# Six contraction groups instead of nine, with every accumulation on VectorE, and weight tiles split in one step of 2048 columns

## Chip, cores and metric

The kernel runs on one core of a Trainium2 chip. The metric is device time in microseconds of one execution of the whole layer, as the median of several runs. A profiled execution of its own gives the trace.

## What is computed

One layer of a streaming encoder on x of 256 tokens by 2048 columns, all in float32: a feed-forward block (FFN 1), a mixer of two attention branches, a second feed-forward block (FFN 2) and a last norm. Each of the three blocks has a norm ahead of it whose scale and shift, and a gate whose size, come from a vector c through one large matrix (`w_ada`, 2048 by 9 x 2048). The part that matters here is FFN 1:

```python
mod = (jax.nn.silu(c) @ w_ada[i] + b_ada[i]).reshape(B, N_MOD, D)
sh1, sc1, ga1, sh2, sc2, ga2, sh3, sc3, ga3 = [mod[:, j, None, :] for j in range(N_MOD)]
h = _rms_norm(x, g_ffn1[i]) * (1.0 + sc1) + sh1
x = x + 0.5 * ga1 * _swiglu(h, w1_a[i], w3_a[i], w2_a[i])     # (silu(h @ w1) * (h @ w3)) @ w2, D_FF = 5632
```

So h needs two of the nine parts of `mod` before its first row can be used, and w1 and w3 (2048 by 5632 each) are read once from HBM.

## The kernel before

**Exact products.** Every weight tile and every left operand is split into a high part that TensorE's float32r takes without loss and a remainder. `split_raw` (lines 87 to 102) does this for weights: ScalarE (ACT) copies a piece of the raw tile into `wh` (line 97), VectorE (DVE) subtracts it from the raw tile into `wl` (line 98). A tile of 2048 columns is taken in two pieces of 1024, each in buffers of its own; the pool `hl` has six of each kind. `mm3` (lines 108 to 111) then adds three products into PSUM: high by high (109), high by remainder (110), remainder by high (111). One "unit" of weights is 128 partitions by 2048 columns, 1 MB: four rows of tiles of 512 columns, for two blocks of 128 tokens, so 24 products of 128 by 512.

**Loads.** Raw tiles come through SyncE's (SP's) DMA queue into three buffers of 2048 columns (pool `raws`), in order. A buffer is free when its last reader is done: for a weight tile the DVE subtraction.

**Modulation.** `mod` is computed on DVE beside all this: an ada unit (lines 159 to 164) loads 1 MB of `w_ada` into a raw buffer, multiplies it by silu(c) and sums each row (line 163), which gives one column of one of the nine parts. `mod_cols` (201 to 213) turns columns into the scale and shift of the norm with three tiny DVE operations (208, 210, 212). `fill` issues queued ada units, `need` all up to a given one.

**The prologue of FFN 1** (lines 396 to 513). The first 6 of 11 chunks of 512 columns of w1 and w3 are done while `mod` is still arriving. The contraction over the 16 row tiles of h is cut into groups: `GROUPS = (1, 1) + (2,) * 7`. A group's rows of h^T are built when its ada units are done (`xn_T`, `mod_T`; the remainder of h is subtracted on GpSimd (POOL) here, line 312 with `early`). Then for each chunk and each of w1, w3 the group's products go into a PSUM tile `pacc`, one of two (`psA`), and from there into a running sum in SBUF, `sum`. That is 12 partial sums per group of 128 by 1024 elements, 108 in all:

- group 0: ACT stores the 12 sums (line 496);
- later groups: every third is added by DVE straight from PSUM (line 503); for the others ACT copies PSUM to `ev` (507) and POOL adds `ev` to `sum` (508), 56 in all;
- last group: the sum of w1 goes by ACT and POOL (500, 501) and then through silu on ACT (510), the sum of w3 by DVE, and POOL multiplies the two (512).

A raw tile of the prologue holds four slots of 512 columns, so 48 tiles in all. `AHEAD` says how many raw tiles ahead of its group the ada units of that group are issued; between these marks `target` spreads them evenly. 37 ada units belong to the prologue. Behind it `RATE = 0.75` ada units are issued per weight unit until the queue is empty.

**After the prologue** FFN 1 goes on with `ffn_down` for the six chunks, `ffn_up` and `ffn_down` for the other five (lines 515 to 523), then mixer and FFN 2. All of them take their weights through `gemm`, `unit_parts` and `split_raw`.

**What sets the order.** The source gives an order, and the framework that builds the program puts the instructions of each engine into a queue in the order in which they become ready by its own reckoning, those earlier in the source first; semaphores enforce the data's order. The queues are fixed when the program is built, and each engine works through its own strictly in that order.

Of the kernel before, what the change touches and what calls it, by code (L numbers as in the profile page):

```python
# [32 lines left out]
# offsets of the columns of `cols`  # L33
C_BADA, C_GF1, C_GMX, C_GF2, C_GQL, C_GKV, C_GQN, C_GKN = 0, 144, 160, 176, 192, 196, 200, 201
# offsets of the parts of `rows`
# [4 lines left out]
def layer_kernel(ctx: ExitStack, tc: tile.TileContext, a: dict):  # L40
# [6 lines left out]
    hl = ctx.enter_context(tc.tile_pool(name="hl", bufs=6, reuse_waits="tile"))  # L47
# [10 lines left out]
    def wkA(name):  # L58
        return wk.tile([P, 1024], F32, tag="wA", name=name)
# [4 lines left out]
    # ------------------------------------------------------------ constants  # L64
# [16 lines left out]
    # ------------------------------------------------------------ weights  # L81
# [5 lines left out]
    def split_raw(raw, src_cols, n):  # L87
        """exact parts of raw[:, :src_cols], as pairs of n columns"""
        res = []
        per = max(1, (src_cols // n) // 2)  # L90
        k = 0
        while k * n < src_cols:
            w = min(per * n, src_cols - k * n)
            wh = hl.tile([P, 1024], F32R, tag="wh", name="wh")
            wl = hl.tile([P, 1024], F32R, tag="wl", name="wl")
            src = raw[:, k * n:k * n + w]
            ACT.copy(wh[:, :w], src)  # L97
            DVE.tensor_tensor(wl[:, :w], src, wh[:, :w].bitcast(F32), op=ALU.subtract)  # L98
            for q in range(w // n):
                res.append((wh[:, q * n:(q + 1) * n], wl[:, q * n:(q + 1) * n]))  # L100
            k += w // n
        return res

    def unit_parts(ap, nkt, n):
        """one weight unit: nkt tiles of n columns"""
        return split_raw(load_unit(ap, nkt * n), nkt * n, n)
# [8 lines left out]
    def gemm(acc, units, n=512, tbm=None, mid=None, hook=None):  # L115
        """acc[tok, n] = x^T W over the units (ap, nkt, k0, xs); units tbm[0]:tbm[1] are
        done for one token block and then for the other"""
        total = sum(u[1] for u in units)
        tbm = tbm or (0, 0)
        i = 0  # L120
        held = []

        def run(tb, parts, i, xs, k0):
            for j, (wh, wl) in enumerate(parts):
                xh, xl = xs(k0 + j, tb)
                out = acc[tb][:, :n] if isinstance(acc, list) else acc[:, tb, :n]
                mm3(out, xh, xl, wh, wl, start=(i + j == 0), stop=(i + j == total - 1))

        for ui, (ap, nkt, k0, xs) in enumerate(units):
            if hook and ui in hook:  # L130
                hook[ui]()
            parts = unit_parts(ap, nkt, n)
            if tbm[0] <= ui < tbm[1]:
                held.append((parts, i, xs, k0))
                run(0, *held[-1])
                if ui == tbm[1] - 1:
                    if mid:
                        mid()
                    for h in held:
                        run(1, *h)  # L140
            else:
                for j, part in enumerate(parts):
                    if hook and j > 0 and ui + j / nkt in hook:
                        hook[ui + j / nkt]()
                    for tb in range(TB):
                        run(tb, [part], i + j, xs, k0 + j)
            i += nkt
            rate[1] += rate[0]
            while rate[1] >= 1.0:
                fill(1)  # L150
                rate[1] -= 1.0
        if hook and len(units) in hook:
            hook[len(units)]()

    # ------------------------------------------------------------ adaLN columns
# [15 lines left out]
    def need(j, kt):  # L171
        """issue what is queued up to the unit that gives column kt of mod j"""
        while (j, kt) not in ada_done:
            fill(1)
# [7 lines left out]
    def load_c(pool, first=False):  # L182
        """silu(c) on every partition"""
        c_bc = pool.tile([P, D], F32, tag="cbc", name="c_bc")
        if not first:
            ACT.dma_start(c_bc, a["c"].to_broadcast([P, D]))
            ACT.activation(c_bc, c_bc, AF.Silu)
            return c_bc
        SP.dma_start(c_bc[0:1, :], a["c"])
        ACT.activation(mod[:, 0:16], mhalf, AF.Silu)  # L190
        ps = bank("warm")
        for _ in range(WARM):
            PE.matmul(ps[:, 0:P], ones, ones, start=True, stop=True)
        ACT.activation(c_bc[0:1, :], c_bc[0:1, :], AF.Silu)
        for kg in range(4):
            ps = bank("c_ps")
            PE.matmul(ps, ones[0:1, :], c_bc[0:1, kg * 512:(kg + 1) * 512], start=True, stop=True)
            ACT.copy(c_bc[:, kg * 512:(kg + 1) * 512], ps)
        return c_bc

    def mod_cols(i, lo, hi, c_g):
        """columns lo:hi of (a, b) of norm i"""
# [12 lines left out]
    def gate_rows(pool, i, scale, name):  # L215
        """gate i as rows broadcast over the partitions, 512 columns at a time"""
# [25 lines left out]
    # ------------------------------------------------------------ norm into T layout  # L242
# [24 lines left out]
    def next_hT(i):  # L267
        """a list that takes h^T of norm i, and what fills it for a token block"""
        hT = []

        def then(tb):
            hT.append(new_hT_tb(tb))
            for kg in range(4):
                norm_T(hT, i, tb, kg * 4, 4)
        return hT, then
# [7 lines left out]
    def norm_T(hT, i, tb, k0, nk):  # L283
        """rows k0*128.. of h^T of norm i, in exact parts"""
        mod_T(hT, i, tb, k0, nk, xn_T(tb, k0, nk))
# [10 lines left out]
    def mod_T(hT, i, tb, k0, nk, ps, early=False):  # L296
# [15 lines left out]
        (POOL if early else DVE).tensor_tensor(lo, hv, hi.bitcast(F32), op=ALU.subtract)  # L312

    # ------------------------------------------------------------ FFN
    def ffn_act(acc1, acc3):
        """silu(acc1) * acc3"""
# [7 lines left out]
    def ffn_gT(g, ring, name):  # L324
        """g transposed, in exact parts: [P, 2, 4, S]"""
# [13 lines left out]
    def resid(acc, g, n, tbs, tail=False, then=None):  # L339
        """x += acc * gate for the 512 columns n of the token blocks tbs"""  # L340
# [13 lines left out]
    def add_product(units, g, n, tail, then, tbm, hook=None):  # L354
        """x += gate * (product) for the 512 columns n"""
# [39 lines left out]
    # ================================================================ FFN 1  # L395
    NPRO = 6
    GROUPS = (1, 1) + (2,) * 7
    ADD_DVE = 3
    LEAD = 3
    XLEAD = 1  # L400
    AHEAD = lambda gi: (0, 1, 0, 1, 2, 3, 4, 5, 5)[gi]
# [3 lines left out]
    with tc.tile_pool(name="f1", bufs=1, reuse_waits="tile") as f1, \  # L405
# [37 lines left out]
        # ada units that have to be issued before a raw tile  # L443
# [14 lines left out]
        for r, grp in enumerate(raws_of):  # L458
# [21 lines left out]
            for sl, part in zip(grp, split_raw(raw, len(grp) * 512, 512)):  # L480
                parts[sl] = part
            for gi, c, wi, k in grp:
# [12 lines left out]
                if gi == 0:  # L495
                    ACT.copy(sums[c][:, wi], acc)
                elif gi == len(GROUPS) - 1 and wi == 0:
                    pre = wkA("silu")
                    pv = pre.rearrange("p (t n) -> p t n", t=TB)
                    ACT.copy(pv, acc)  # L500
                    POOL.tensor_tensor(pv, pv, sums[c][:, 0], op=ALU.add)
                elif (c * 2 + wi) % ADD_DVE == 0 or gi == len(GROUPS) - 1:
                    DVE.tensor_tensor(sums[c][:, wi], acc, sums[c][:, wi], op=ALU.add)  # L503
                else:
                    ev = wkB("ev")
                    evv = ev.rearrange("p (t n) -> p t n", t=TB)
                    ACT.copy(evv, acc)  # L507
                    POOL.tensor_tensor(sums[c][:, wi], sums[c][:, wi], evv, op=ALU.add)  # L508
                if gi == len(GROUPS) - 1 and wi == 1:
                    ACT.activation(pre, pre, AF.Silu)  # L510
                    g = wkB("gact")
                    POOL.tensor_tensor(g, sums[c][:, 1].rearrange("p t n -> p (t n)"), pre, op=ALU.mult)
                    late.append(g)
# [12 lines left out]
    # ================================================================ mixer  # L526
# [16 lines left out]
    with tc.tile_pool(name="mx", bufs=1, reuse_waits="tile") as mx:  # L543
# [4 lines left out]
        with tc.tile_pool(name="mla", bufs=1, reuse_waits="tile") as ml:  # L548
            # ---- rotary tables
# [68 lines left out]
            # ---- latents  # L618
            def latent(parts, c_g, name):
                """RMS-normed latent, transposed, in exact parts; parts: per token block 512 columns"""  # L620
# [38 lines left out]
            # query latent, k_rope and g_lr: columns [q 0:256 | k_rope], [q 256:512 | g_lr]  # L659
# [13 lines left out]
            # ---- k_rope | g_lr  # L673
            def rope(dst, src, tab, nh):
                """dst, src [P, TB, nh, 64]"""
# [39 lines left out]
            def mla_pair(hp, k_hook):  # L715
                """latents up for two heads; returns the stages of their attention"""
# [136 lines left out]
        with tc.tile_pool(name="late", bufs=1, reuse_waits="tile") as lt, ExitStack() as ctx2:  # L853
# [5 lines left out]
            with tc.tile_pool(name="gla", bufs=1, reuse_waits="tile") as gl:  # L859
# [38 lines left out]
                def gla_head(h, hook):  # L898
                    """one head; returns the stages behind its projections"""
# [147 lines left out]
    # ================================================================ FFN 2  # L1047
# [37 lines left out]
def _units(w):  # L1085
    """[K, N] -> [K/512, N/512, 128, 4*512]: 512x512 blocks, rows k*128+p at partition p"""
# [59 lines left out]
```

## Time and profile before

| | us |
|---|---|
| median of 3 runs | 2260.61 |
| lowest and highest | 2259.78, 2260.78 |
| span of the profiled execution, first to last instruction | 2255.0 |
| prologue's products (`pacc`), first start to last start | 19.0 to 402.6 |
| TensorE, busy | 2161.3 (96%) |
| VectorE, busy | 1578.9 (70%) |
| ScalarE, busy | 1044.3 (46%) |
| GpSimd, busy | 276.6 (12%) |

The profiled execution is known by its span; what lies around a span counts in the runs' time. Busy time of TensorE is that of pipelined products and not a measure of its peak: the number of products in a window of time says more. Names: PE is TensorE, PEld its weight loads, DVE VectorE, ACT ScalarE, POOL GpSimd, SP SyncE. A group of instructions is named by line, engine, operation and by the tiles that it writes and reads; then come the count, the busy time, the mean duration in ns, and the idle time ahead of them with what ended it.

### The profile page before, as it was taken

To read this page: it belongs to the slowest core of one execution; us is meant where nothing else is said; L and a number is where in the kernel's file an instruction comes from. 1 tells how busy PE (TensorE), PEld (TensorE's weight loads), DVE (VectorE), ACT (ScalarE), POOL (GpSimd) and SP (SyncE) were. 2 spreads that over 40 slices of the span, in tenths; PEclk is the share of its full clock that TensorE was granted. 3 is DMA by queue.
4 is the path that set the end of the run, shared out by engine and by line. 5 is a ranking of instruction groups with operands and counts; after the bars stand their busy time and mean duration, and the time that the engine had idled before them with its cause. 6 is when DMAs were issued, how large, how long until landed. Compare 5 with 4: busy or idle time off the path is not lost.

```text
span 2255.0 us, 24933 instructions
## 1 busy us (share of the span) xinstructions
PE 2161.3 (96%) x9652; PEld 1763.1 (78%) x9652; DVE 1578.9 (70%) x1604; ACT 1044.3 (46%) x1279; POOL 276.6 (12%) x148
## 2 busy tenths in 40 slices
PE   8788788999999999999999999999999999999998
PEld 5566566788888887988777788878888888888886
DVE  6999898888787787756566667766666455444454
ACT  6545455433433445555564444455444433444443
POOL 1766557100000000001000000000000000000000
PEclk8899899999999999999999999999999999999999
DMA  8667675799898884644576777866777555555553
GB/s 297 230 233 253 227 248 192 276 352 347 334 336 324 328 318 148 227 145 165 195 256 245 257 262 278 296 235 241 281 287 268 191 208 196 189 193 187 194 189 112
DMA packets 87305, 549.16 MB, mean 244 GB/s; under 512 B 10322, under 2 KB 10626, under 8 KB 28435
## 3 DMA queue, kind: packets, MB, share of 16 engines
q1 hardware_dynamic: 84242, 539.97, 66.4%
q0 software_dynamic: 1344, 3.17, 0.5%
q10 hardware_dynamic: 1602, 4.44, 0.5%
q8 instruction: 75, 1.23, 0.2%
q14 instruction: 42, 0.34, 0.0%
HBM read 545.42 MB, written 2.12 MB: 243 GB/s over the span
## 4 chain that ended last, share of the span: by engine, by line
PE 82%; DVE 7%; issue 4%; DMA 3%; POOL 2%; ACT 1%; SPq 0%; POOLq 0%; DVEq 0%; ACTq 0%
PE a L109 10%; PE a L111 10%; PE a L110 10%; PE y L111 8%; PE y L110 8%; PE y L109 8%; DVE wl L98 3%; DMA raw<-in_w_a 2%; DVE raw L163 2%; POOL sum L508 1%; PE qkv L109 1%; PE ga L109 1%; PE gb L109 1%; PE ga L111 1%; PE qkv L111 1%
## 5 line engine op out<-in xcount | busy, mean ns | idle before, releaser
L98 DVE TENSOR_TENSOR wl<-raw,wh 128x1024 fp32r<-128x1024 f32 (+1 forms) x744 | 959.3, 1305 | 522.8 <-ACT wh L97 520.7
L97 ACT CAST wh<-raw 128x1024 fp32r<-128x1024 f32 (+1 forms) x744 | 765.5, 1042 | 965.2 <-PE a L111 283.7
L109 PE MATMUL a<-wh,hTh 128*128 128x512 f32 x1024 | 399.8, 390 | 0.3 <-ACT hTh L311 0.3
L111 PE MATMUL a<-wh,hTl 128*128 128x512 f32 x1024 | 399.0, 390 | 0.0
L110 PE MATMUL a<-wl,hTh 128*128 128x512 f32 x1024 | 398.6, 389 | 0.0
L163 DVE SCALAR_TENSOR_TENSOR raw<-raw,c_bc 128x2048 f32<-128x2048 f32 x144 | 351.1, 2438 | 38.1 <-DMA raw<-in_w_ada 37.7
L109 PE MATMUL y<-wh,gT 128*128 128x512 f32 x704 | 275.1, 391 | 0.0
L111 PE MATMUL y<-wh,gT 128*128 128x512 f32 x704 | 274.2, 389 | 0.0
L110 PE MATMUL y<-wl,gT 128*128 128x512 f32 x704 | 274.2, 389 | 0.0
L111 PEld LDWEIGHTS a<-wh,hTl 128*128 128x128 f32 x1024 | 192.2, 188 | 41.0 <-DVE hTl L312 0.8
L109 PEld LDWEIGHTS a<-wh,hTh 128*128 128x128 f32 x1024 | 192.3, 188 | 39.9 <-ACT hTh L311 0.6
L110 PEld LDWEIGHTS a<-wl,hTh 128*128 128x128 f32 x1024 | 192.3, 188 | 39.3
L109 PE MATMUL pacc<-wh,hTh 128*128 128x512 f32 x384 | 166.7, 434 | 56.0 <-DVE sum L503 50.1
L508 POOL TENSOR_TENSOR sum<-sum,ev 128x1024 f32<-128x1024 f32 x56 | 172.6, 3093 | 121.2 <-ACT ev L507 121.1
L110 PE MATMUL pacc<-wl,hTh 128*128 128x512 f32 x384 | 163.0, 424 | 11.3 <-DVE wl L98 11.3
L111 PE MATMUL pacc<-wh,hTl 128*128 128x512 f32 x384 | 161.0, 419 | 1.7 <-POOL hTl L312 1.7
L109 PEld LDWEIGHTS y<-wh,gT 128*128 128x128 f32 x704 | 132.2, 188 | 28.1
L111 PEld LDWEIGHTS y<-wh,gT 128*128 128x128 f32 x704 | 132.2, 188 | 27.3
L110 PEld LDWEIGHTS y<-wl,gT 128*128 128x128 f32 x704 | 132.2, 188 | 27.2
L109 PEld LDWEIGHTS pacc<-wh,hTh 128*128 128x128 f32 x384 | 79.4, 207 | 86.2 <-DVE sum L503 53.4
L507 ACT COPY ev<-pacc 128x1024 f32<-128x1024 f32 x56 | 56.8, 1014 | 106.1 <-PE pacc L111 100.6
L110 PEld LDWEIGHTS pacc<-wl,hTh 128*128 128x128 f32 x384 | 79.7, 207 | 29.9 <-DVE wl L98 13.8
(296 smaller groups left out, 2487.6 us busy)
## 6 DMA issues: line engine op xcount, KB each, us to landing
raw<-in_w_ada SPq DMA_DIRECT2D x144, 1024.0 KB, 5.2
raw<-in_w_b SPq DMA_DIRECT2D x132, 1024.0 KB, 4.8
raw<-in_w_a SPq DMA_DIRECT2D x84, 1024.0 KB, 5.8
raw<-in_w_in SPq DMA_DIRECT2D x60, 1024.0 KB, 4.8
raw<-in_w_a SPq DMA_DIRECT2D x84, 512.0 KB, 5.0
raw<-in_w_out SPq DMA_DIRECT2D x16, 1024.0 KB, 5.6
raw<-in_w_proj_a SPq DMA_DIRECT2D x8, 1024.0 KB, 4.9
raw<-in_w_proj_b SPq DMA_DIRECT2D x8, 1024.0 KB, 4.8
```

The lines of the kernel that those rows point to most:

```text
L97: ACT.copy(wh[:, :w], src)
L98: DVE.tensor_tensor(wl[:, :w], src, wh[:, :w].bitcast(F32), op=ALU.subtract)
L109: PE.matmul(out, xh, wh, start=start, stop=False)
L110: PE.matmul(out, xh, wl, start=False, stop=False)
L111: PE.matmul(out, xl, wh, start=False, stop=stop)
L163: DVE.scalar_tensor_tensor(out=raw, in0=raw, scalar=1.0, in1=c_bc, op0=ALU.mult, op1=ALU.mult, accum_out=dst)
L507: ACT.copy(evv, acc)
L508: POOL.tensor_tensor(sums[c][:, wi], sums[c][:, wi], evv, op=ALU.add)
```

## The change

Three things change together.

The groups become `(1, 1, 2, 4, 4, 4)`, with marks of their own for the ada units. The 48 raw tiles stay 48, the products stay the same in number; the partial sums fall from 108 to 72.

All partial sums behind group 0 are added by DVE straight from PSUM. In the last group, silu follows on ACT, and the product with it is DVE's. The remainder of h in the prologue is DVE's too. No tensor operation of the prologue is left on POOL but the powers of the norm.

`split_raw` takes one buffer pair of 2048 columns for a raw tile, three of each kind instead of six of half the size (the same memory), and splits it in one step: one ACT copy and one DVE subtraction of all its columns. Only the raw tiles of the first three groups are split in two steps, into that one buffer pair. This holds for all weights of the kernel.

```diff
-    hl = ctx.enter_context(tc.tile_pool(name="hl", bufs=6, reuse_waits="tile"))
+    hl = ctx.enter_context(tc.tile_pool(name="hl", bufs=3, reuse_waits="tile"))
...
-    def split_raw(raw, src_cols, n):
-        """exact parts of raw[:, :src_cols], as pairs of n columns"""
-        res = []
-        per = max(1, (src_cols // n) // 2)
-        k = 0
-        while k * n < src_cols:
-            w = min(per * n, src_cols - k * n)
-            wh = hl.tile([P, 1024], F32R, tag="wh", name="wh")
-            wl = hl.tile([P, 1024], F32R, tag="wl", name="wl")
-            src = raw[:, k * n:k * n + w]
-            ACT.copy(wh[:, :w], src)
-            DVE.tensor_tensor(wl[:, :w], src, wh[:, :w].bitcast(F32), op=ALU.subtract)
-            for q in range(w // n):
-                res.append((wh[:, q * n:(q + 1) * n], wl[:, q * n:(q + 1) * n]))
-            k += w // n
-        return res
+    def split_raw(raw, src_cols, n, steps=1):
+
+        wh = hl.tile([P, 2048], F32R, tag="wh", name="wh")
+        wl = hl.tile([P, 2048], F32R, tag="wl", name="wl")
+        w = src_cols // steps
+        for c in range(0, src_cols, w):
+            src = raw[:, c:c + w]
+            ACT.copy(wh[:, c:c + w], src)
+            DVE.tensor_tensor(wl[:, c:c + w], src, wh[:, c:c + w].bitcast(F32), op=ALU.subtract)
+        return [(wh[:, c:c + n], wl[:, c:c + n]) for c in range(0, src_cols, n)]
...
-        (POOL if early else DVE).tensor_tensor(lo, hv, hi.bitcast(F32), op=ALU.subtract)
+        DVE.tensor_tensor(lo, hv, hi.bitcast(F32), op=ALU.subtract)
...
-    GROUPS = (1, 1) + (2,) * 7
-    ADD_DVE = 3
+    GROUPS = (1, 1, 2, 4, 4, 4)
...
-    AHEAD = lambda gi: (0, 1, 0, 1, 2, 3, 4, 5, 5)[gi]
+    AHEAD = lambda gi: (0, 1, 1, 2, 4, 5)[gi]
...
-            for sl, part in zip(grp, split_raw(raw, len(grp) * 512, 512)):
+            for sl, part in zip(grp, split_raw(raw, len(grp) * 512, 512, 2 if GROUPS[grp[0][0]] < 4 else 1)):
...
-                elif gi == len(GROUPS) - 1 and wi == 0:
-                    pre = wkA("silu")
-                    pv = pre.rearrange("p (t n) -> p t n", t=TB)
-                    ACT.copy(pv, acc)
-                    POOL.tensor_tensor(pv, pv, sums[c][:, 0], op=ALU.add)
-                elif (c * 2 + wi) % ADD_DVE == 0 or gi == len(GROUPS) - 1:
-                    DVE.tensor_tensor(sums[c][:, wi], acc, sums[c][:, wi], op=ALU.add)
-                else:
-                    ev = wkB("ev")
-                    evv = ev.rearrange("p (t n) -> p t n", t=TB)
-                    ACT.copy(evv, acc)
-                    POOL.tensor_tensor(sums[c][:, wi], sums[c][:, wi], evv, op=ALU.add)
-                if gi == len(GROUPS) - 1 and wi == 1:
-                    ACT.activation(pre, pre, AF.Silu)
-                    g = wkB("gact")
-                    POOL.tensor_tensor(g, sums[c][:, 1].rearrange("p t n -> p (t n)"), pre, op=ALU.mult)
-                    late.append(g)
+                    continue
+                DVE.tensor_tensor(sums[c][:, wi], acc, sums[c][:, wi], op=ALU.add)
+                if gi == len(GROUPS) - 1:
+                    if wi == 0:
+                        pre = wkA("silu")
+                        ACT.activation(pre, sums[c][:, 0].rearrange("p t n -> p (t n)"), AF.Silu)
+                    else:
+                        g = wkB("gact")
+                        DVE.tensor_tensor(g, sums[c][:, 1].rearrange("p t n -> p (t n)"), pre, op=ALU.mult)
+                        late.append(g)
```

## The prediction

> **What bounds the kernel now.** The page comes first, for the shape of the run.
>
> ```profile
> span 2255.0 us, 24933 instructions
> ...
> PE   8788788999999999999999999999999999999998
> DVE  6999898888787787756566667766666455444454
> ...
> POOL 1766557100000000001000000000000000000000
> PEclk8899899999999999999999999999999999999999
> ```
>
> A slice is 56 us. After slice 7, PE is busy in full. Only in the first seven slices, the prologue that the change rewrites, is PE below that, while DVE is nearly full and POOL is in use, as almost nowhere later. A time table by stage says how far PE is from its best there.
>
> ```profile
> 300.00:350.00 50.00, 41.02 (x154) 32.46 (x155) 47.97 (x33) 24.03 (x29) 28.52 (x11) 0.88 0.70 237
> 500.00:550.00 50.00, 50.00 (x223) 41.28 (x222) 42.17 (x38) 19.18 (x20) 1.09 (x2) 1.00 0.92 355
> 850.00:900.00 50.00, 47.21 (x228) 37.90 (x226) 34.57 (x78) 30.83 (x56) 2.80 (x3) 1.00 0.40 136
> ```
>
> Columns: PE, PEld, DVE, ACT, POOL, each busy us with its count, then clock, DMA share, GB/s. A full window holds 223 products, one per 50 / 223 = 0.224 us; the prologue's window holds 154. DVE is busy 48 of 50 us there. The second window is the stage after the prologue: PE is full, but DMA is at 0.92 and 355 GB/s. Next come the groups of the first 410 us, by form.
>
> ```profile
> L98 DVE TENSOR_TENSOR wl<-raw,wh 128x1024 fp32r<-128x1024 f32 x101 | 191.4, 1922 | 23.2 <-ACT wh L97 23.1
> L508 POOL TENSOR_TENSOR sum<-sum,ev 128x1024 f32<-128x1024 f32 x56 | 172.6, 3093 | 121.2 <-ACT ev L507 121.1
> L109 PE MATMUL pacc<-wh,hTh 128*128 128x512 f32 x384 | 166.7, 434 | 56.0 <-DVE sum L503 50.1 <-ACT ev L507 4.2 <-ACT sum L496 0.9
> ...
> L163 DVE SCALAR_TENSOR_TENSOR raw<-raw,c_bc 128x2048 f32<-128x2048 f32 x38 | 108.7, 2861 | 5.9 <-DMA raw<-in_w_ada 5.8
> ...
> L503 DVE TENSOR_TENSOR sum<-pacc,sum 128x1024 f32<-128x1024 f32 x34 | 41.2, 1213 | 4.4 <-PE pacc L111 4.4
> ...
> L208 DVE TENSOR_TENSOR ab<-mod,small 128x2 f32<-128x2 f32 x7 | 10.4, 1484 | 0.1
> L212 DVE SCALAR_TENSOR_TENSOR ab<-modt,small 128x2 f32<-128x2 f32 x7 | 7.6, 1084 | 0.2
> ...
> L210 DVE TENSOR_TENSOR modt<-mod,small 128x2 f32<-128x2 f32 x7 | 5.4, 766 | 0.1
> ...
> L210 DVE TENSOR_TENSOR modt<-mod,small 128x1 f32<-128x1 f32 x2 | 0.3, 160 | 0.1
> ```
>
> PE's first product of a sum (L109) waits 50.1 us for DVE's addition, while DVE itself waits for little: 23.2 + 5.9 + 4.4 = 33.5 us. So DVE bounds the prologue. The odd part is its prices: a column operation on two elements takes up to 1.5 us where a like one, early on, takes 0.16. The lines of three instructions, first the split in the prologue, then split and modulation product (ada unit) after it, then the addition:
>
> ```profile
> L98 DVE TENSOR_TENSOR wl<-raw,wh x101: 1207/1227/3429, 17.9 to 407.9; 128x1024 fp32r<-128x1024 f32 x101
> ```
>
> ```profile
> L98 DVE TENSOR_TENSOR wl<-raw,wh x158: 1214/1219/1227, 419.4 to 848.1; 128x1024 fp32r<-128x1024 f32 x158
> ```
>
> ```profile
> L163 DVE SCALAR_TENSOR_TENSOR raw<-raw,c_bc x57: 2280/2284/2294, 424.0 to 832.8; 128x2048 f32<-128x2048 f32 x57
> ```
>
> ```profile
> L111 PE MATMUL pacc<-wh,hTl x384: 387/389/797, 20.1 to 402.6; 128*128 128x512 f32 x192
> ...
> L503 DVE TENSOR_TENSOR sum<-pacc,sum x34: 1209/1211/1225, 46.1 to 405.6; 128x1024 f32<-128x1024 f32 x34
> ```
>
> Durations are least/median/most in ns. Where POOL is idle, the split takes 1.22 us without exception; where POOL works, up to 3.43, which is the split plus most of a POOL addition (3.09 on average). The addition, which reads PSUM and one SBUF tile, never stretches (1.21 to 1.23) in the same stretch of time. I read this as POOL's additions holding up those DVE instructions that read two SBUF tiles.
>
> The Trainium skill, "SBUF — State Buffer", section "Who interferes with whom", states just that: DVE with two SBUF inputs and a GpSimd instruction that reads SBUF exclude each other, and the later one blocks in full. The trace agrees (3.43 against 1.22, and 1.21 flat for one SBUF input).
>
> **The prologue, part by part.** It lasts from 19 to 403 us, 384 us.
>
> (a) POOL's work goes: 56 sums, 6 + 6 of the last group, 18 remainders of h. The waits that it puts on DVE go with it: splits 191.4 - 101 x 1.22 = 68; ada units 108.7 - 38 x 2.284 = 22; columns 10.4 + 7.6 + 5.4 - 21 x 0.16 = 20. Together 110 us of DVE. What stays on POOL, the powers of the norms and the gate rows' DMAs behind the prologue, only loses predecessors.
>
> (b) DVE takes over. Six groups instead of nine leave 12 x 6 = 72 sums, 12 of them stored by ACT as now, 60 added on DVE: 26 more than the 34 now, at 1.21: 31.5 us. ACT's 56 evictions go as well; it was not the bound. The product with silu, 6 instructions:
>
> ```profile
> L321 DVE TENSOR_TENSOR gact<-a,silu 128x1024 f32<-128x1024 f32 x16 | 19.6, 1224 | 5.6 <-PE a L111 5.6
> ...
> L312 DVE TENSOR_TENSOR hTl<-hf,hTh 128x512 fp32r<-128x512 f32 x16 | 10.6, 685 | 2.4 <-ACT hTh L311 2.2
> ```
>
> 6 x 1.22 = 7.3. Remainders of h: 12 instructions over 4096 columns, between 8 x 0.685 = 5.5 by columns and 12 x 0.685 = 8.2 by count; I take 6. Sum added: 45.
>
> (c) Wide splits. A 2048-column split is not in the trace. Above stand two halves, 2.44 us; the nearest row is the ada unit, 2.284, of this width with two SBUF inputs. I take that: 36 wide tiles save 36 x 0.15 = 5.5. Three groups fewer save 9 column operations, 1.4.
>
> DVE then has 110 - 45 + 7 = 72 us less. If it waits as long as now, the prologue shortens by 72, to 312 us. PE needs 1152 products x 0.224 = 258 of these, so 83% where it is 67% now; the 48 + 37 tiles of 1.05 MB would need 286 GB/s where 355 are shown. With three engines near their limits waits grow: for a tile of the four-deep groups, PE needs 24 x 0.224 = 5.4 us and DVE 2.28 + 1.21 + half an ada unit 1.18 = 4.7, plus the small things. I add a third of today's DVE waits, 12 us; the ends are a third less and twice as much. **Prologue: -60 (from -84 to -38).**
>
> **After the prologue.** Between 420 and 850 us, every unit of four rows needs its own tile and about 0.7 of an ada tile from three buffers. Here is what SP's queue waits for, and how long tiles take to land when DMA is loaded (w_a) and when it is not (w_b).
>
> ```profile
> SPq L84 <- DVE wl L98: 239.8, 78, 5.7
> SPq L84 <- DVE raw L163: 121.2, 54, 7.0
> ```
>
> ```profile
> raw<-in_w_b SPq DMA_DIRECT2D x132, 1024.0 KB, 4.8
> raw<-in_w_a SPq DMA_DIRECT2D x84, 1024.0 KB, 5.8
> ```
>
> ```profile
> L97 ACT CAST wh<-raw 128x1024 fp32r<-128x1024 f32 x720 | 748.0, 1052 | 945.5 <-PE a L111 283.7 <-DMA raw<-in_w_a 241.1 <-PE y L111 180.3
> ```
>
> SP stands 361 of 430 us waiting for DVE to release a tile, so the loads run at the pace of the three buffers. A weight tile is released after half a copy and two half splits, 1.05 + 2.44 = 3.5 us; in one step it is a whole copy and a whole split. The copy of 2048 columns, which no row shows, takes more than one half, 1.05, and at most two, 2.10; near the upper end, as splits go by their columns. With 2.28 behind it that is 4.4 us at most: a weight tile is held up to 0.9 us longer. 158 half splits are 79 weight tiles, beside 57 ada tiles (the second and third of the lines above): 0.9 x 79 / 136 = 0.52 us in the mean, a third of it per transfer, x 136 = 24 us if nothing gives way. The lower end, a copy no longer than a half, would be a gain in holding (3.3 us against 3.5), which PE, full already, could not use: 0. What gives way: landing takes 5.8 us in this load and 4.8 without, so a thinner queue gives back up to 1.0 us, more than is lost; and PE is not short of anything here today. From 0 to 24, I take 8.
>
> Elsewhere DMA has room and PE's cover is thinner by half a tile. Where a chain of small steps runs between two stages (the window at 850 us, PE 47.2 of 50), ACT and DVE finish a piece of 2.1 to 2.3 us before they turn to it, not one of 1.05 to 1.22: half a microsecond more in the mean, at some four meetings. +2 (0 to 6).
>
> **Sum.** Against the profiled execution: 2255.0 - 60 + 8 + 2 = 2205 us of span. The median of the runs, 2260.6, is 5.6 above this span; that stays: 2210.6.
>
> **Rivals.**
>
> *Additions in the way (slower).* Every addition now stands on DVE and waits for PE. If the split of the next tile is queued behind the addition of the present one, PE and DVE take turns: 5.4 + 1.21 + 2.28 + 1.18 = 10.1 us for each of the 36 wide tiles, where the forecast has 324 / 48 = 6.75. That is +120, so 2331 us; from 15 of the 36 on (50 / 3.35) nothing is left of the gain. For it: the source has the steps in just this order. Against it: instructions do not stand on DVE as they do in the source.
>
> ```profile
> 188.37 3.48 DVE L98 TENSOR_TENSOR wl<-raw,wh 128x1024 fp32r<-128x1024 f32 x3
> 192.51 1.23 DVE L503 TENSOR_TENSOR sum<-pacc,sum 128x1024 f32<-128x1024 f32 x1 [0.66 <-PE pacc L111]
> ```
>
> Three half splits run before an addition that waits for PE: they are for later products. Three tiles of 2048 columns hold as many columns as six of 1024, so two tiles can lie ahead. Chance 0.15, mostly for parts of it.
>
> *Starved by the buffers.* The coarser release costs its full 24, the chains 6, and the prologue's waits double: -38 + 30 = -8, 2253 us. For it: SP's waits. Against it: the landing times. 0.10.
>
> *A slower PE clock.* The prologue has products of 797 ns beside 387 (the L111 line above) and a clock of 0.88. Waits for a whole tile are longer pieces of idleness; if a third of the products ran at half speed, PE alone would need 258 x 1.33 = 343 us, -41 instead of -60: 2230. The Trainium skill, "TensorE: Matmul & The Clock Gate", Part 1, says that an idle window of about 3.4 us halves the clock; by that rule a PE that waits more rarely would be faster, not slower. 0.03.
>
> *It does not do what it says.* If POOL is not what stretches DVE's instructions, 110 us stay and the added 45 come on top: -60 + 110 + 10 = +60, 2321 us. The flat 1.21 of the addition speaks against it. 0.02.
>
> **How the numbers follow.** The forecast has 0.70: about 2211, by itself from 2178 to 2248. The buffers' rival (0.10) lies at the upper end; both slower rivals (0.17) and a rest below are left out: 2178 to 2255. Some 0.2% (4.5 us) can be told from no change: the runs before lie within 1.0 us. Faster 0.70 + 0.03 + 0.06 of the buffers' rival = 0.79; same 0.04; slower 0.15 + 0.02 = 0.17.
>
> **What would show it.** The prologue's last product at about 343 us, not 403; splits of 2.28 us without stretched ones; column operations of 0.16 us; POOL empty; DVE still the busiest there. Additions found waiting for PE for long, with PE waiting for the split behind them, would show the first rival; PE below 50 of 50 us in the stage behind the prologue, with ACT waiting for DMA, the second. If splits stay stretched with POOL empty, the reading of the cause is wrong.

## The result, and the profile after

| | before | after |
|---|---|---|
| median of runs, us | 2260.2 (4 runs, 2259.13 to 2260.78) | 2207.6 (4 runs, 2202.86 to 2217.67) |
| ratio to before | 1 | 0.9768, 95% interval 0.9744 to 0.9793 |
| span of the profiled execution, us | 2255.0 | 2207.1 |

The change makes the kernel 2.3% faster. The page of the changed kernel, the same lines as before:

```profile
span 2207.1 us, 23664 instructions
...
PE   7799999999999989999999999999999999999998
...
DVE  7989887777777767555566677666665455444454
...
POOL 0000000000000000100000000000000000000000
PEclk9899999999999999999999999999999999999999
```

In the prologue PE is below nine tenths in two slices, not in seven, and POOL is empty; a new dent shows in slice 15. The tile `pacc`, its last product and the additions:

```profile
L105 PE MATMUL pacc<-wh,hTl x384: 387/389/629, 20.0 to 331.9; 128*128 128x512 f32 x192
L491 DVE TENSOR_TENSOR sum<-pacc,sum x60: 1208/1219/1225, 44.5 to 332.4; 128x1024 f32<-128x1024 f32 x60
```

The prologue's last product starts at 331.9 us instead of 402.6. Here are the groups up to 334 us, by form.

```profile
L95 DVE TENSOR_TENSOR wl<-raw,wh 128x2048 fp32r<-128x2048 f32 x38 | 87.0, 2288 | 14.0 <-ACT wh L94 13.8
L157 DVE SCALAR_TENSOR_TENSOR raw<-raw,c_bc 128x2048 f32<-128x2048 f32 x37 | 84.5, 2284 | 4.8 <-DMA raw<-in_w_ada 4.7
...
L491 DVE TENSOR_TENSOR sum<-pacc,sum 128x1024 f32<-128x1024 f32 x60 | 72.6, 1219 | 14.3 <-PE pacc L105 14.1
L95 DVE TENSOR_TENSOR wl<-raw,wh 128x1024 fp32r<-128x1024 f32 x24 | 28.8, 1218 | 3.6 <-ACT wh L94 3.6
...
L204 DVE TENSOR_TENSOR modt<-mod,small 128x4 f32<-128x4 f32 x3 | 0.5, 153 | 0.0
```

Nothing is stretched any more: the ada unit has 2.284 on average (2.861 before), the column operation 0.153 (0.766), the half split 1.218 (1.922). The wide split, which no row showed before, takes 2.288. DVE's waits in these four groups are 14.0 + 4.8 + 14.3 + 3.6 = 36.7 us, where the three of before had 33.5. Time by stage:

```profile
200.00:250.00 50.00, 49.45 (x217) 40.31 (x216) 45.25 (x35) 22.85 (x20) 0.00 (x0) 1.00 0.85 312
...
450.00:500.00 50.00, 49.51 (x218) 40.44 (x217) 36.65 (x24) 18.14 (x10) 0.00 (x0) 1.00 0.89 329
...
750.00:800.00 50.00, 47.22 (x200) 38.25 (x200) 33.54 (x26) 17.73 (x16) 0.00 (x0) 0.97 0.79 291
800.00:850.00 50.00, 44.59 (x226) 34.99 (x225) 38.85 (x108) 31.84 (x51) 1.81 (x3) 1.00 0.30 97
```

In the last part of the prologue PE now runs 217 products in 50 us, nearly the 223 of a full window. But the stage behind it, full before, now has 218, and the two windows around 800 us have PE busy for 47.2 and 44.6 of 50 us.

Behind the prologue, PE takes the products in the same order in all kernels of this study, but for six that change places between the 1173rd and the 1178th in after, wide_only and less_wide, and four there in dve_halves. So one can look up in each trace when PE starts the k-th (from 0) of the 2976 products with the low part of the weights; those of FFN 1 end with the 1055th. Differences to the kernel before, in us of their profiled executions:

| kernel | first behind the prologue (384th) | first of the mixer (1056th) | early in the mixer (1248th) | last (2975th) |
|---|---|---|---|---|
| after | -70.7 | -59.4 | -50.1 | -48.1 |
| groups_only | -74.7 | -74.7 | -74.8 | -74.1 |
| wide_only | +0.8 | +10.3 | +21.3 | +23.2 |
| nine_dve | -48.9 | -33.8 | -33.6 | -33.6 |
| two_steps | -71.5 | -71.4 | -70.0 | -69.4 |
| act_halves | -70.5 | -58.4 | -54.8 | -50.5 |
| dve_halves | -67.1 | -50.1 | -45.6 | -45.4 |
| less_wide | -70.3 | -69.4 | -60.3 | -57.3 |
| less_half | -71.0 | -70.9 | -70.1 | -70.1 |
| six_pool | -45.1 | -43.4 | -43.5 | -43.5 |
| pool_reads | -13.5 | -13.6 | -13.5 | -13.5 |
| pool_writes | -74.5 | -74.1 | -74.2 | -73.4 |

The changed kernel gains 70.7 us in the prologue and gives back 22.6 behind it: 11.3 up to the mixer's first product, 9.3 in the first part of the mixer, 2.0 in the rest.

### The profile page after: what moved, and what is told of

Its sections match the earlier page's. It is cut to its first block, busy times and chain, and to the rows that moved or that the text cites. A ratio compares the mean times of both kernels' runs of the same rounds, so it can differ in the third digit from the quotient of the medians.

```text
span 2207.1 us, 23664 instructions
## 1 busy us (share of the span) xinstructions
PE 2147.0 (97%) x9652; PEld 1749.7 (79%) x9652; DVE 1469.9 (67%) x1279; ACT 928.8 (42%) x845; POOL 39.0 (2%) x62
## 4 chain that ended last, share of the span: by engine, by line
PE 74%; DMA 9%; DVE 9%; ACT 4%; issue 3%; POOL 0%; SPq 0%; ACTq 0%; POOLq 0%; DVEq 0%
PE a L105 8%; PE a L104 8%; PE a L103 8%; DMA raw<-in_w_a 7%; PE y L105 6%; PE y L104 6%; PE y L103 6%; DVE wl L95 4%; ACT wh L94 3%; DVE raw L157 3%; PE pacc L104 2%; PE pacc L105 2%; PE pacc L103 2%; DMA raw<-in_w_ada 2%; PE qkv L103 1%
## 5 line engine op out<-in xcount | busy, mean ns | idle before, releaser
L95 DVE TENSOR_TENSOR wl<-raw,wh 128x2048 fp32r<-128x2048 f32 (+3 forms) x384 | 844.1, 2199 | 557.9 <-ACT wh L94 557.2
L94 ACT CAST wh<-raw 128x2048 fp32r<-128x2048 f32 (+3 forms) x384 | 705.8, 1839 | 1131.4 <-DMA raw<-in_w_a 392.8
L157 DVE SCALAR_TENSOR_TENSOR raw<-raw,c_bc 128x2048 f32<-128x2048 f32 x144 | 329.1, 2285 | 25.4 <-DMA raw<-in_w_ada 25.2
L103 PE MATMUL pacc<-wh,hTh 128*128 128x512 f32 x384 | 156.3, 407 | 14.5 <-ACT wh L94 8.7
L104 PE MATMUL pacc<-wl,hTh 128*128 128x512 f32 x384 | 155.9, 406 | 11.0 <-DVE wl L95 10.7
L105 PE MATMUL pacc<-wh,hTl 128*128 128x512 f32 x384 | 153.8, 400 | 0.0
L103 PEld LDWEIGHTS pacc<-wh,hTh 128*128 128x128 f32 x384 | 74.2, 193 | 36.7 <-ACT wh L94 10.8
L104 PEld LDWEIGHTS pacc<-wl,hTh 128*128 128x128 f32 x384 | 74.7, 194 | 32.2 <-DVE wl L95 17.1
L105 PEld LDWEIGHTS pacc<-wh,hTl 128*128 128x128 f32 x384 | 74.7, 194 | 15.4
L491 DVE TENSOR_TENSOR sum<-pacc,sum 128x1024 f32<-128x1024 f32 x60 | 72.6, 1219 | 14.3 <-PE pacc L105 14.1
```

The lines of the kernel that those rows point to most:

```text
L94: ACT.copy(wh[:, c:c + w], src)
L95: DVE.tensor_tensor(wl[:, c:c + w], src, wh[:, c:c + w].bitcast(F32), op=ALU.subtract)
L103: PE.matmul(out, xh, wh, start=start, stop=False)
L104: PE.matmul(out, xh, wl, start=False, stop=False)
L105: PE.matmul(out, xl, wh, start=False, stop=stop)
L157: DVE.scalar_tensor_tensor(out=raw, in0=raw, scalar=1.0, in1=c_bc, op0=ALU.mult, op1=ALU.mult, accum_out=dst)
```

## The experiments

Theory A: POOL's additions held up DVE, DVE bounds the prologue, and the wide split only costs. Rival B: the smaller number of sums is the gain. Rival C: the wide split is part of it.

**groups_only**: the two parts of the change kept apart.

```diff
-        wh = hl.tile([P, 2048], F32R, tag="wh", name="wh")
-        wl = hl.tile([P, 2048], F32R, tag="wl", name="wl")
...
+            wh = hl.tile([P, 1024], F32R, tag="wh", name="wh")
+            wl = hl.tile([P, 1024], F32R, tag="wl", name="wl")
```

(`split_raw` and the six buffers of before, all else as after.)

> The changed kernel with the split of before: two halves of 1024 columns in six buffers; groups 1,1,2,4,4,4 and all additions on DVE stay. Theory A (POOL's additions held up DVE, DVE bounds the prologue, the wide split only costs later): prologue's last product at 330 to 340 us, nothing lost behind it, so 2260 - 70 = about 2190 us, faster than the changed kernel by 15 to 20. Rival C (the wide split is a good part of the gain in the prologue): prologue's end at 350 or later, 2205 us or more.

Measured: 2182.55 us median (5 runs, 2181.13 to 2187.59), ratio to before 0.9656 (0.9643 to 0.967). It is the fastest kernel here, by 25 us ahead of the changed one. The last products of its prologue:

```profile
L111 PE MATMUL pacc<-wh,hTl x384: 387/389/628, 20.0 to 327.9; 128*128 128x512 f32 x192
```

The prologue is 4 us shorter with half splits, and next to nothing (0.6 us) is lost behind it. Rival C falls. The 4 us themselves are not firm: less_half, with the same splits and buffers but other ada units at the prologue's end, has -71.0 in the table, as the changed kernel has.

**wide_only**: the other part alone, on the kernel before.

```diff
-    hl = ctx.enter_context(tc.tile_pool(name="hl", bufs=6, reuse_waits="tile"))
+    hl = ctx.enter_context(tc.tile_pool(name="hl", bufs=3, reuse_waits="tile"))
...
+    def split_raw(raw, src_cols, n, steps=1):
```

> The kernel before with only the split changed: wide buffers, three of them, one step behind the prologue, two steps within it (all its groups are under four rows deep). Theory A: the prologue stays at its 403 us within 10 us, since POOL's additions stay; behind it the 20 to 25 us are lost that the changed kernel loses there, so 2280 to 2290 us. Rival C: a gain in the prologue, 2250 us or less.

Measured: 2277.17 us (4 runs), ratio 1.007 (1.0053 to 1.0087): 0.7% slower, 3 us less than theory A's range has. In its prologue, whose groups have one or two rows, every tile is split in two steps, so this run tests the one-step split behind the prologue only. The prologue stays (+0.8 us), 22.4 us are lost behind it, as much as in the changed kernel. There the one-step split is a loss by itself, and the same loss with or without the other part.

**nine_dve**: nine groups, no addition on POOL.

```diff
-    GROUPS = (1, 1, 2, 4, 4, 4)
+    GROUPS = (1, 1) + (2,) * 7
```

(on groups_only, with the marks of before)

> Groups 1,1,2,2,2,2,2,2,2 as before, half splits as before, but all 96 additions, the remainders of h and the product with silu on DVE and none on POOL. Theory A: the 110 us of stretched DVE instructions go, 62 additions of 1.21 us and 13 us of other work come, so DVE has 22 us less and the kernel takes about 2240 us (2225 to 2255). Rival B (the number of partial sums is what counts, POOL does not hold up DVE): DVE gets 62 x 1.21 + 13 = 88 us more, 2320 us or more.

Measured: 2220.11 us (4 runs), ratio 0.982 (0.9806 to 0.9833). Groups up to 410 us:

```profile
L98 DVE TENSOR_TENSOR wl<-raw,wh 128x1024 fp32r<-128x1024 f32 x116 | 138.5, 1216 | 13.3 <-ACT wh L97 13.2
L497 DVE TENSOR_TENSOR sum<-pacc,sum 128x1024 f32<-128x1024 f32 x96 | 115.9, 1218 | 11.1 <-PE pacc L111 10.8
```

DVE does 62 additions more and the kernel is faster all the same (1.8%), because the split is back at 1.216. Rival B in its strict form falls. The gain is larger than was expected, 48.9 us in the prologue where 22 were; of this DVE's waits give 12.4 (from 19 us to the prologue's end it is idle 20.3 us, 32.7 before). Its busy time there falls by 36.5 us (352.4 to 315.9) where 22 were expected; some 8 of the difference are work that it has not done yet at that point, three half splits and two ada units, and the rest was not followed up. And though it splits in halves, it gives back 15 us up to the mixer's first product. In that stretch its splits are ready 2 us ahead of PE in the median, those of groups_only 8 to 9. So time is lost there without any wide split too.

**six_pool**: the groups alone.

```diff
-    GROUPS = (1, 1) + (2,) * 7
+    GROUPS = (1, 1, 2, 4, 4, 4)
```

(on the kernel before, with the marks of after)

> The kernel before with the groups 1,1,2,4,4,4 alone: a third of the additions on DVE, the others by ACT and POOL, half splits. POOL's tensor operations fall from 234 to about 161 us. Theory A: three parts in ten of the 110 us of held-up DVE instructions go, 34 us, and 12 additions on DVE fewer, 15 us: about 2212 us (2195 to 2230). Rival B (the number of sums counts, whoever adds them): as groups_only, 2183 us.

Measured: 2214.74 us (4 runs), ratio 0.9799 (0.9783 to 0.9815), 2.7 above theory A's figure. Up to 410 us:

```profile
L98 DVE TENSOR_TENSOR wl<-raw,wh 128x1024 fp32r<-128x1024 f32 x116 | 179.3, 1576 | 40.3 <-ACT wh L97 40.3
L163 DVE SCALAR_TENSOR_TENSOR raw<-raw,c_bc 128x2048 f32<-128x2048 f32 x43 | 121.8, 2837 | 15.8 <-DMA raw<-in_w_ada 15.8
L508 POOL TENSOR_TENSOR sum<-sum,ev 128x1024 f32<-128x1024 f32 x32 | 93.2, 2915 | 141.2 <-ACT ev L507 141.1
```

With fewer POOL additions the split is stretched less (1.576, not 1.922; 1.616 for the 99 of the prologue alone, which ends at 357 us here). So groups alone bring 45 us in the prologue, no POOL alone 49, both together 75: they overlap, since fewer sums also means fewer POOL additions.

**pool_reads and pool_writes**: the disputed mechanism by itself.

```diff
+        spare = f1.tile([P, 512], F32, name="spare")
+        for q in range(112):
+            POOL.tensor_tensor(spare, x_sb[:, 0, 0:512], x_sb[:, 1, 0:512], op=ALU.add)
```

(on groups_only; pool_writes has 320 times `POOL.memset(spare, 1.0)` instead)

> Six groups, half splits, all additions on DVE (the kernel of groups_only, 2183 us), plus work on POOL that nobody waits for: 112 additions of two stretches of 512 columns of x in SBUF into a spare tile, about 1.5 us each by half of the 3.09 us row, 170 us in all, free to run from the start of the prologue. Theory A: splits and ada units are stretched while it lasts; before, 234 us of POOL's tensor operations gave 110 us of DVE waiting, so some 80 us here (40 to 110), nearly all of it on the path: 2225 to 2290 us. If POOL does not hold up DVE: 2183 us within 5.

> The same, but the extra POOL work only writes: 320 fills of 512 columns of the spare tile, some 0.5 us each, 160 us in all. If it is POOL's reading of SBUF that holds up DVE's instructions with two SBUF inputs, nothing changes: 2183 us within 5, splits at 1.22 us. If any POOL work does, as in pool_reads: 2220 us or more.

Measured: pool_reads 2243.52 us (4 runs), ratio 0.993 (0.9915 to 0.9945); pool_writes 2184.65 us (4 runs), ratio 0.967 (0.9654 to 0.9686). The groups up to 334 us, pool_reads first:

```profile
L458 POOL TENSOR_TENSOR spare<-x_sb 128x512 f32<-128x512 f32 x112 | 247.2, 2207 | 15.9 <-DMA x_sb<-in_x 7.3
L98 DVE TENSOR_TENSOR wl<-raw,wh 128x1024 fp32r<-128x1024 f32 x82 | 130.7, 1621 | 9.7 <-ACT wh L97 9.7
...
L163 DVE SCALAR_TENSOR_TENSOR raw<-raw,c_bc 128x2048 f32<-128x2048 f32 x34 | 99.5, 2925 | 0.0
L500 DVE TENSOR_TENSOR sum<-pacc,sum 128x1024 f32<-128x1024 f32 x50 | 60.2, 1214 | 4.5 <-PE pacc L111 4.3
```

```profile
L458 POOL MEMSET spare<- 128x512 f32 x320 | 168.6, 527 | 18.3
...
L98 DVE TENSOR_TENSOR wl<-raw,wh 128x1024 fp32r<-128x1024 f32 x102 | 122.1, 1219 | 13.5 <-ACT wh L97 13.0
...
L163 DVE SCALAR_TENSOR_TENSOR raw<-raw,c_bc 128x2048 f32<-128x2048 f32 x38 | 86.8, 2283 | 2.9 <-DMA raw<-in_w_ada 1.6 <-ACT c_bc L198 1.4
L500 DVE TENSOR_TENSOR sum<-pacc,sum 128x1024 f32<-128x1024 f32 x60 | 72.6, 1219 | 14.1 <-PE pacc L111 13.8
```

The split's least, median and most in ns, again pool_reads first:

```profile
L98 DVE TENSOR_TENSOR wl<-raw,wh x81: 1205/1224/2316, 27.2 to 329.8; 128x1024 fp32r<-128x1024 f32 x81
```

```profile
L98 DVE TENSOR_TENSOR wl<-raw,wh x102: 1211/1218/1226, 17.8 to 329.7; 128x1024 fp32r<-128x1024 f32 x102
```

Work on POOL that no one waits for costs 61 us if it reads SBUF: splits 1.621, ada units 2.925, and the addition with one operand in PSUM stays at 1.214. Work that only writes costs nothing measurable, with 169 us of it. A fill is shorter than an addition (0.53 against 2.2 us), but not one of the 102 splits beside the fills takes more than 1.226 us, so the difference is not one of length alone. Some 9 of the 61 us are another cause: the second block's power of the norm stands in POOL's queue behind six of the extra additions and starts at 23.2 us, and the prologue's first product starts at 28.1 us instead of 18.9. That POOL's additions, which read SBUF, hold up DVE's instructions with two SBUF operands, and its fills do not, is thus shown, not only argued. The Trainium skill, "SBUF — State Buffer", section "Who interferes with whom", draws the same line between a GpSimd instruction that reads SBUF and one that only writes it; these two runs agree with it (61 us and 2).

**two_steps, act_halves, dve_halves**: what the loss behind the prologue is.

```diff
-        return split_raw(load_unit(ap, nkt * n), nkt * n, n)
+        return split_raw(load_unit(ap, nkt * n), nkt * n, n, 2)
```

(two_steps, the prologue's call likewise; the other two take the halves for ACT's copy or DVE's subtraction alone. All have the three wide buffers.)

> The changed kernel with every tile split in two steps, but into the same three wide buffers. It tells apart what the loss behind the prologue (23 us) comes from. If the length of a piece on ACT and DVE counts (1.9 and 2.3 us instead of 1.05 and 1.22): most of the loss comes back, about 2190 us. If the coarser release of the split buffers counts: it stays, 2200 to 2210 us.

> The changed kernel, but ACT copies every weight tile in two halves; DVE subtracts it in one step as in the change, in the same three wide buffers. With both engines in halves 2187 us, with neither 2208. If the long pieces of ACT are what the small steps between the stages queue behind: most of the 20 us come back, 2187 to 2193. If those of DVE: little, 2203 to 2208. If both alike: about 2197.

> The mirror image: ACT copies a weight tile in one step, DVE subtracts it in two halves. If DVE's long pieces are what counts: 2187 to 2193 us. If ACT's: 2203 to 2208. If both alike: about 2197.

Measured: two_steps 2187.3 us (4 runs, ratio 0.967, 0.9657 to 0.9683), act_halves 2203.48 (4 runs, 0.975, 0.9733 to 0.9768), dve_halves 2212.11 (4 runs, 0.9783, 0.9763 to 0.9802). Halves on both engines bring nearly all of the loss back; halves on either engine alone bring back little or nothing. That was none of the three cases in the expectations. The effects do not add because a piece is not all that changes. With halves on both, DVE works on the first half while ACT copies the second: a raw tile is free 1.05 + 2 x 1.22 = 3.5 us after its copy starts. In the other three it is 1.91 + 2.29 = 4.2 (after), 2.10 + 2.29 = 4.4 (act_halves), 1.91 + 2.44 = 4.35 (dve_halves): ACT and DVE work one after the other. The traces bear this out: over the first 64 weight tiles behind the prologue the medians are 3.44, 4.24, 4.32 and 4.31 us. In the table, up to the mixer's first product, two_steps loses 0.1 us, the other three 11.3, 12.1 and 17.0. The coarser split buffers as such cost little: two_steps and groups_only are 4.7 us apart, and their intervals meet.

**less_wide and less_half**: is it the load on the raw buffers?

```diff
+    POOL.memset(mod, 0.0)
...
-            ada_q.append(lambda kt=kt: ada_unit(c_bc, j, kt))
+            if j in (2, 3, 4, 5) and kt % 2:
+                ada_q.append(lambda kt=kt: ada_done.add((j, kt)))
+            else:
+                ada_q.append(lambda kt=kt: ada_unit(c_bc, j, kt))
```

> The changed kernel with every second ada unit of parts 2 to 5 of the modulation left out (its column is zero), so that behind the prologue about half as many ada tiles share the three raw buffers. To be read against less_half, the same with half splits in six buffers. With all ada units the wide split costs 25 us (4 in the prologue, 21 behind it). If that is because a weight tile holds its raw buffer longer while loads run at the pace of the three buffers: with the load relieved, little is left of the 21, and the two kernels differ by 4 to 9 us. If the long pieces themselves stand in the way of the small steps between FFN 1 and mixer: the difference stays at 19 to 25 us.

> The kernel of groups_only (six groups, additions on DVE, half splits in six buffers) with the same ada units left out: PE was full behind the prologue there already, so 2175 to 2183 us by either theory.

Measured: less_wide 2199.57 us (4 runs, ratio 0.9728, 0.9714 to 0.9743), less_half 2186.51 (4 runs, 0.9671, 0.9656 to 0.9685). They differ by 13.1 us, between the two theories. less_half itself is 3.5 us above its expected range. It is 4.0 us slower than groups_only, and the table has 3.7 of these at the prologue's end already. Two long windows behind the prologue, first of the changed kernel, then of less_wide:

```profile
340.00:500.00 160.00, 158.75 (x702) 129.90 (x701) 120.81 (x87) 54.93 (x34) 3.29 (x6) 1.00 0.88 328
500.00:750.00 250.00, 248.66 (x1111) 204.57 (x1110) 191.92 (x134) 96.12 (x63) 0.00 (x0) 1.00 0.88 328
```

```profile
340.00:500.00 160.00, 160.00 (x713) 132.23 (x712) 100.95 (x67) 58.77 (x36) 3.30 (x6) 1.00 0.74 273
500.00:750.00 250.00, 250.00 (x1124) 207.43 (x1123) 158.53 (x102) 97.64 (x68) 0.00 (x0) 1.00 0.70 261
```

With the load at 273 and 261 GB/s instead of 328, the wide split feeds PE in full: 713 and 1124 products, not 702 and 1111. Up to the mixer's first product less_wide loses 0.9 us, so 10 of the changed kernel's 11.3 need the load. With the load as it is, two_steps, which holds a raw tile 0.8 us less, loses 0.1: this points at the raw buffers. Fewer ada units also relieve DVE and the DMA, and halves also bring the first split of a tile to PE sooner; these were not separated from the holding. Of the 11.3 us, 5.0 fall at one place:

```profile
773.37 1.90 ACT L94 CAST wh<-raw 128x2048 fp32r<-128x2048 f32 x1 [7.72 <-DMA raw<-in_w_a]
...
775.33 0.73 PE L103 MATMUL y<-wh,gT 128*128 128x512 f32 x2 [0.85 <-ACT wh L94]
775.65 2.28 DVE L95 TENSOR_TENSOR wl<-raw,wh 128x2048 fp32r<-128x2048 f32 x1
...
777.99 0.50 PE L104 MATMUL y<-wl,gT 128*128 128x512 f32 x1 [1.93 <-DVE wl L95]
```

The tile lands late: ACT has waited 7.72 us for it. Copy and split one after the other then take 4.6 us, and PE waits 0.85 us for the copy and 1.93 for the split. groups_only, whose splits run ahead, has no such wait. Behind it the clock comes down: from 779.5 us on it is granted 0.50 for 3.4 us, which makes another 1.7 of the 5.0. nine_dve stalls at the same place (3.26 us) for another reason: a step of the residual stands ahead of the split in DVE's queue and waits 3.40 us for PE.

In the first part of the mixer less_wide loses 9.1, as the changed kernel does (9.3). So there are two causes, each about half. The second begins to show in the changed kernel's order of time where the mixer's norm is made, just ahead of the 1056th product (810.2 us):

```profile
803.00 1.89 ACT L94 CAST wh<-raw 128x2048 fp32r<-128x2048 f32 x1
...
804.80 0.79 ACT L300 ACTIVATE hf<-xT,ab 128x128 f32<-128x128 f32 x2
804.93 2.29 DVE L95 TENSOR_TENSOR wl<-raw,wh 128x2048 fp32r<-128x2048 f32 x1 [0.60 <-ACT wh L94]
...
807.14 0.72 DVE L297 TENSOR_SCALAR hf<-xT,ab 128x128 f32<-128x128 f32 x2
808.51 0.81 ACT L300 ACTIVATE hf<-xT,ab 128x128 f32<-128x128 f32 x2
808.65 2.29 DVE L95 TENSOR_TENSOR wl<-raw,wh 128x2048 fp32r<-128x2048 f32 x1 [0.80 <-ACT wh L94]
```

The norm's steps of 0.4 us (`hf`) start when a copy of 1.9 or a split of 2.3 ends, on both engines. The mixer's first 32 products, which wait for this norm, take 2.8 of the 9.3 us. The largest single loss, 4.0 us from the 1168th to the 1200th, stands in the steps that make the queries of the attention:

```profile
893.08 2.28 DVE L95 TENSOR_TENSOR wl<-raw,wh 128x2048 fp32r<-128x2048 f32 x1
895.28 0.42 DVE L666 TENSOR_TENSOR rp<-qx,ta 128x256 f32<-128x256 f32 x1
...
896.02 2.29 DVE L95 TENSOR_TENSOR wl<-raw,wh 128x2048 fp32r<-128x2048 f32 x1
898.22 0.42 DVE L669 TENSOR_TENSOR qx<-rp,rp 128x256 f32<-128x256 f32 x1
...
898.78 0.89 PE L758 MATMUL qpT_ps<-small,qx 128*64 128x128 f32 x4 [1.97 <-DVE qx L669]
```

Two wide splits stand between the short steps, and PE waits 1.97 us for the last of them; behind the wait the clock is granted at half for 3.4 us once more, from 899.0 on. In groups_only two splits of 1.22 us stand at the same places, and PE does not wait. The six products that change places (named above the table) lie just there; dve_halves, where four do, loses 0.4 us between the same two products, so their order alone is not the cause. In this part halves on one engine do help: from the 1056th to the 1248th product act_halves loses 3.6, dve_halves 4.5, two_steps 1.4. Whether a fourth raw buffer would cure the first cause was not tried.

## Why the prediction was right, and where it was not

The forecast was 2210.6 us, the median is 2207.6. That it is this close is in part luck: two errors cancel, a gain 10.7 us too small in the prologue and a loss 12.6 us too small behind it.

**The cause (a)** is right, and shown by nine_dve, pool_reads and pool_writes: splits, ada units and column operations are back at 1.22, 2.28 and 0.15 us.

**DVE's additions and the wide split (b, c)** are right as prices. The nearest row for the wide split, 2.284, was within 0.2% of it (2.288). But that it would save time in the prologue is wrong: groups_only, without it, is 4 us faster there. The 0.15 us per tile do show in DVE's busy time from 19 us to the prologue's end (277.1 us, in groups_only 281.0), but its waits are 8.0 us longer (37.3, in groups_only 29.3).

**The prologue: -60 was too small, -70.7 was measured.** The bookkeeping of DVE alone gave -72. The failed step is "I add a third of today's DVE waits, 12 us": they grew from 33.5 to 36.7, 3 us. Over all its instructions from 19 us to the prologue's end, DVE is busy 352.4 us before and 277.1 after, and idle 32.7 and 37.3: 75.3 us less work and 4.6 more waiting, which make the 70.7. Why the waits grew so little with three engines near their limits was not tested.

**After the prologue: +10 was too small, +22.6 was measured.** The buffers were put at 8 of at most 24, and the stretch took 11.3, of which 5.0 are the one stall at 775 us; the mechanism, a tile held longer (4.24 against 3.45 us), fits less_wide and the three kernels with halves. The mis-sized term is the chain of small steps: "some four meetings", 2 us and 6 at most, took 9.3 in the first part of the mixer and 2.0 more behind it. There are more than four meetings, and the forecast had no term for the clock, which after a wait of 2 us there was granted at half for 3.4 us. The pieces' length and not a thin lead of the splits is what counts here: less_wide comes with splits 6.7 us ahead of PE and loses 9.1 all the same, while nine_dve, with half splits and a lead of 2 us, loses 0.2.

**What lies around the span.** The forecast kept 5.6 us between span and median. The profiled execution after has 2208.92 us for a span of 2207.1, so 1.8 lie around it, and in all runs on record it is 1.7 to 2.6. So the larger part of the 5.6 was an execution some 4 us faster than the median, by this estimate, and no fixed cost. The gains in the table, counted from that execution, come out smaller than those of the medians by as much: 48.1 against 52.6 us for the changed kernel. The forecast's own range, 2178 to 2248, is also narrower than the plain sums of the ends of its terms, 2177 to 2253; the result lies well within both.

**The rivals.** Additions in the way did not come true: DVE waits 14.1 us for PE in the whole prologue. The clock of PE in the prologue rose instead of falling: it is 1.00 from 150 to 750 us, where before it was 0.88 in the window at 300 us. Behind that it is granted at half twice, for 3.4 us at 779.5 and at 899.0 us, after waits of 1.93 and 1.97 us and not after a whole idle window of 3.4 us. The starved buffers came true in part, as the forecast's own term. Against the full rival, its prologue did not lose anything.

## What to carry to other kernels

Where VectorE bounds a stage, look at the spread of one instruction's durations before moving work off it: if instructions with two SBUF operands are stretched while GpSimd reads SBUF, the offloaded work can cost more than it saves. Here nine_dve took it all back, 62 additions among it, and was 1.8% faster. Halving a copy-and-subtract pair over two engines was worth its extra instructions here, since the second engine starts after half the time, the landing buffer comes free earlier, and small steps of other chains wait for shorter pieces; undoing it on either engine alone already cost 16 to 25 us against two_steps. A change with several parts is worth taking apart even if it gains: here one part alone gives 78 us (0.9656) and the other takes back 25.

## What the runs showed that was not expected

A lead of the splits is lost more easily than one would think. For each split behind the prologue one can take from the trace how long before PE's first product with it it is ready. In the changed kernel the median is 5.9 us just behind the prologue (340 to 380 us) and 2.3 already between 380 and 420; then it stays between 0.7 and 2.3 up to 620 us, and PE stalls now and then. In wide_only it falls from 11.5 (380 to 420 us) to 0.2 (580 to 620). nine_dve comes with 2 and stays there. The kernel before and groups_only come with 10 to 12 and keep 7 to 9.5 over most of the stage. A lead can also come back: in six_pool it falls to 2.3 (580 to 620 us) and is 8.6 between 700 and 740. Why it does there and not in nine_dve was not followed up.

The times of such kernels also scatter more: 2202.86 to 2217.67 for the changed kernel and 2271.59 to 2281.81 for wide_only in four runs each, against 2256.25 to 2262.99 for all 27 runs of the kernel before. Differences of a few microseconds among act_halves, dve_halves and the changed kernel mean little for that reason.
